# Gate and up products of both feed-forward stages as seven block products for eight, and a down product over all eight PSUM banks

## The chip, the cores and the metric

The kernel runs on one core of one Trainium2 chip. The metric is the device time of one execution in microseconds (us). Engines are called as the profile calls them: PE is TensorE, PEld its weight loads, DVE VectorE, ACT ScalarE, POOL GpSimd, SP the engine whose queue starts the transfers. A difference of less than 0.3% of the time (3.3 us) can't be told from none.

## The reference

One residual block on 512 tokens of width 1024: a feed-forward stage, a mixer of two kinds, and a second feed-forward stage. The change touches both feed-forward stages.

```
D_MODEL = 1024; SEQ = 512; D_FF = 2816
def swiglu(x, w_gu, w_down):
    gu = x @ w_gu                               # (512 x 1024) @ (1024 x 5632)
    gate, up = gu[..., :D_FF], gu[..., D_FF:]
    return (jax.nn.silu(gate) * up) @ w_down    # (512 x 2816) @ (2816 x 1024)

x = x + 1/2 * post1(SwiGLU_1(pre1(x)))
h = pre_mix(x); p = h @ w_in                    # RWKV-7 heads and a conv module on p
x = x + post_mix(concat(A, B) @ w_out)
x = x + 1/2 * post2(SwiGLU_2(pre2(x)))
```

All norms are RMS norms over the 1024 channels with a gain. Everything is float32.

## The kernel before

**Precision by three products.** Every float32 operand of a large product is split into a high part (rounded by ScalarE's cast) and a low part (VectorE: the operand minus its high part). `mm3` (L119) issues three matmuls for a block of 128 contraction rows: high with high (L121), low weight with high (L124), high weight with low (L125). All weights are in DRAM as blocks of 128x1024 float32 (512 KB). `wload` (L80) has SP's queue fetch one, in one fixed order for the whole program; `wblock` (L89) splits it: the cast on ACT (L97), the subtraction on DVE (L100).

**A feed-forward stage** (`ffn`, L286) has gate and up products of 22 column blocks each. The first four blocks (two of gate, two of up) go through `token_halves` (L262), with matmuls over 256 tokens, because the transposed tokens `hT` arrive in pieces. The other 40 blocks have eight contraction steps of three matmuls each, 24 matmuls over all 512 tokens for a block. After a gate and its up block, `tail` takes silu of the gate from PSUM (ACT, L294), multiplies by the up product (DVE, L295) and splits the result into high and low (ACT L297, DVE L298); all 22 split results stay in SBUF in the pool `g`.

**The down product** contracts over 22 blocks of 128. It goes over the tokens' four tiles with 512 output columns at a time: first output half over all 22 blocks, then the second half over 14; the last eight blocks (`NS = 8`) of the second half are done one token tile after the other, so that the tile's post work can start: `Post.piece` takes the sum of squares of a half on ACT (L132) and the scaled half on DVE (L240 to L244), `rs` works out the root on DVE (L49 to L54), and `add` (L251) adds to the residual x. x stays in SBUF. In the first stage the next operand `hT` is transposed tile by tile in between.

**Buffers.** Weight blocks have two raw, two high and two low buffers. Blocks that are fetched ahead of their stage (the first blocks of the mixer, the second half of `w_out`, the first blocks of the second feed-forward stage) have raw buffers of their own: four of tag `raw2`, or a tile of the pool `g`, of which there are 22. PSUM's eight banks are three of A, three of B, two of C and D together.

**Order.** A scheduler orders each engine's instructions at build time, by priorities that follow the program's text; each engine then runs its own list strictly in order. SP's list of weight fetches is fixed by `load` (L72). `w_out` does its first output half, fetches and splits four blocks for the second, posts the first half, fetches and splits the first four blocks of the second feed-forward stage, and then goes over the token tiles.

## Time and profile before

| | |
|---|---|
| median of 3 runs | 1094.14 us (1092.67 to 1096.12) |
| the profiled execution | 1087.74 us |
| its span in the trace | 1085.4 us |
| mean granted clock of TensorE | 0.969 of full speed |
| PE / DVE / ACT / POOL busy | 1030.7 / 530.7 / 408.4 / 147.3 us |
| weights and other data read | 94.50 MB, at 92 GB/s over the span |

The stages in the span, by where their first matmuls start: first feed-forward stage, gate and up, to 256; its down product to about 376, with the turn to the mixer; mixer to about 680; `w_out` to about 715; second stage, gate and up, to 958; its down product to the end. In the two gate and up stretches and in the down products PE is busy the whole time. In a row of a timeline the first number is the start in us and the second the duration; "x2" means that two instructions stand in one row. The end of a matmul is modelled, so the pitch from one start to the next is what is to be read.

### The profile page before, as it was taken

The numbers are of one execution on the slowest core, as the hardware profiler recorded it, in microseconds if no ns is written. First come the engines' busy times: TensorE is split into PE (matmuls) and PEld (weight loads), VectorE is DVE, ScalarE is ACT, GpSimd is POOL, SyncE is SP. The second block draws the span as 40 slices with busy tenths as digits, with TensorE's granted clock in tenths as the row PEclk, the third lists the DMA queues.
The fourth block names the chain that finished last, engine by engine and source line by source line (L and its number), as shares of the span: only waits on it lengthen the run. The fifth ranks groups of instructions, "written<-read, shape, count | busy, mean of one in ns | idle before, by whom it ended". The sixth has DMA issues, their size and how long they took to land.

```text
span 1085.4 us, 15405 instructions
## 1 busy us (share of the span) xinstructions
PE 1030.7 (95%) x6274; PEld 852.5 (79%) x6274; DVE 530.7 (49%) x1011; ACT 408.4 (38%) x628; POOL 147.3 (14%) x170
## 2 busy tenths in 40 slices
PE   8999999999999999859897788999999999999997
PEld 8888888888888797647676666888888888888885
DVE  5333333333224658879469797853333333332225
ACT  7322222222123446765346275543222222221221
POOL 0000000000000234693008280120000000000000
PEclk9999999999999999969896789999999999999999
DMA  6223232333336122121430330502333233333331
GB/s 233 71 89 105 91 103 88 105 90 105 95 97 225 59 72 61 58 70 59 81 98 20 59 118 21 194 20 78 97 98 97 97 97 98 98 97 97 98 116 78
DMA packets 52846, 101.27 MB, mean 93 GB/s; under 512 B 28584, under 2 KB 28712, under 8 KB 52776
## 3 DMA queue, kind: packets, MB, share of 16 engines
q1 hardware_dynamic: 51912, 97.67, 28.7%
q10 hardware_dynamic: 864, 2.63, 0.8%
q8 instruction: 49, 0.80, 0.3%
q14 instruction: 21, 0.17, 0.1%
HBM read 94.50 MB, written 5.78 MB: 92 GB/s over the span
## 4 chain that ended last, share of the span: by engine, by line
PE 72%; DVE 13%; ACT 4%; POOL 4%; DMA 3%; issue 3%; SPq 1%; DVEq 0%; ACTq 0%; POOLq 0%
PE ps L125 23%; PE ps L121 23%; PE ps L124 23%; POOL cacc L516 4%; DVE wlo L100 1%; DVE ps L682 1%; DVE stmp L679 1%; DMA td<-T 1%; DVE x L251 1%; ACT ms_j L132 1%; DMA N<-md 1%; DMA md<-Mt 1%; DVE rs_w L50 1%; ACT cpr L515 1%; ACT whi L97 1%
## 5 line engine op out<-in xcount | busy, mean ns | idle before, releaser
L121 PE MATMUL ps<-hT,whi 128*128 128x512 f32 (+1 forms) x888 | 339.4, 383 | 5.1 <-ACT hT L171 2.8
L124 PE MATMUL ps<-hT,wlo 128*128 128x512 f32 (+1 forms) x888 | 339.3, 382 | 1.5 <-DVE wlo L100 1.1
L125 PE MATMUL ps<-hT,whi 128*128 128x512 f32 (+1 forms) x888 | 339.2, 383 | 1.2 <-DVE hT L172 1.0
L100 DVE TENSOR_TENSOR wlo<-wraw,whi 128x1024 fp32r<-128x1024 f32 x141 | 174.1, 1236 | 318.6 <-ACT whi L97 318.3
L97 ACT CAST whi<-wraw 128x1024 fp32r<-128x1024 f32 x141 | 148.0, 1050 | 301.8 <-PE ps L125 181.4
L121 PEld LDWEIGHTS ps<-hT,whi 128*128 128x128 f32 x888 | 168.6, 190 | 43.5 <-issue 4.8
L125 PEld LDWEIGHTS ps<-hT,whi 128*128 128x128 f32 x888 | 168.3, 190 | 36.6 <-issue 3.7
L124 PEld LDWEIGHTS ps<-hT,wlo 128*128 128x128 f32 x888 | 168.7, 190 | 34.0 <-DVE wlo L100 1.9
L516 POOL TENSOR_TENSOR cacc<-cacc,cpr 128x192 f32<-128x192 f32 (+3 forms) x120 | 116.2, 968 | 46.4 <-ACT cpr L515 38.2
L121 PE MATMUL ps<-whi,g 128*128 128x512 f32 x288 | 112.0, 389 | 0.0
L124 PE MATMUL ps<-whi,g 128*128 128x512 f32 x288 | 112.0, 389 | 0.0
L125 PE MATMUL ps<-wlo,g 128*128 128x512 f32 x288 | 104.4, 389 | 0.0
L294 ACT ACTIVATE sg<-ps 128x512 f32<-128x512 f32 x44 | 26.4, 600 | 166.0 <-PE ps L125 166.0
L295 DVE TENSOR_TENSOR sg<-sg,ps 128x512 f32<-128x512 f32 x44 | 30.3, 688 | 111.5 <-PE ps L125 111.5
L515 ACT ACTIVATE cpr<-gpad,vecs 128x192 f32<-128x192 f32 (+3 forms) x120 | 68.0, 575 | 33.5 <-POOL cacc L516 33.3
L154 POOL TENSOR_TENSOR fg<-x,gain 128x1024 f32<-128x1024 f32 x8 | 19.1, 2388 | 434.7 <-DVE x L251 430.2
L125 PEld LDWEIGHTS ps<-wlo,g 128*128 128x128 f32 x288 | 54.1, 188 | 11.3
L121 PEld LDWEIGHTS ps<-whi,g 128*128 128x128 f32 x288 | 54.1, 188 | 11.3
L124 PEld LDWEIGHTS ps<-whi,g 128*128 128x128 f32 x288 | 54.1, 188 | 11.1
L508 DVE SCALAR_TENSOR_TENSOR ps<-gpad,vecs,ps 128x320 f32<-128x320 f32 (+2 forms) x87 | 40.6, 466 | 1.4
L298 DVE TENSOR_TENSOR g<-sg,g 128x512 fp32r<-128x512 f32 x44 | 30.2, 685 | 1.4 <-ACT g L297 1.4
L297 ACT CAST g<-sg 128x512 fp32r<-128x512 f32 x44 | 27.0, 615 | 5.5 <-DVE sg L295 5.5
(212 smaller groups left out, 1090.6 us busy)
## 6 DMA issues: line engine op xcount, KB each, us to landing
wraw<-w SPq DMA_DIRECT2D x145, 512.0 KB, 3.5
lraw<-w SPq DMA_DIRECT2D x17, 512.0 KB, 5.2
gain<-gains ACTq DMA_DIRECT2D x5, 512.0 KB, 4.5
x<-x SPq DMA_DIRECT2D x4, 512.0 KB, 5.0
xs<-x SPq DMA_DIRECT2D x4, 512.0 KB, 2.7
x<-xs SPq DMA_DIRECT2D x4, 512.0 KB, 7.2
out<-x SPq DMA_DIRECT2D x3, 512.0 KB, 2.6
N<-md SPq DMA_DIRECT2D x4, 256.0 KB, 4.1
```

The costliest lines, as they stand in the source:

```text
L97: c.last_hi = nc.scalar.copy(hi, raw)
L100: c.last_lo = nc.vector.tensor_tensor(lo, raw, hi, ALU.subtract)
L121: i = nc.tensor.matmul(out, lhsT=lh, rhs=rh, start=start, stop=False)
L124: nc.tensor.matmul(out, lhsT=ll, rhs=rh, start=False, stop=False)
L125: return nc.tensor.matmul(out, lhsT=lh, rhs=rl, start=False, stop=stop)
L294: nc.scalar.activation(sg, psg, AF.Silu)
L295: nc.vector.tensor_tensor(sg, sg, psu, ALU.mult)
L297: nc.scalar.copy(g[:, 0], sg)
L298: nc.vector.tensor_tensor(g[:, 1], sg, g[:, 0], ALU.subtract)
L508: self.dve_queue(nc.vector.scalar_tensor_tensor(dst, gp[:, j : j + n], dw[:, j : j + 1], lo, ALU.mult, ALU.add), False)
L515: nc.scalar.mul(pr, gp[:, n + j : j + SEQ], dw[:, j : j + 1])
L516: self.pool_queue(nc.gpsimd.tensor_tensor(hi, hi, pr, ALU.add), j == 1)
```

## The change

**Gate and up.** From the fifth column block on (`LEADF = 4` pairs of gate and up stay as they were, that is the first eight blocks), the blocks go in units of two: a pair of gate blocks, then a pair of up blocks. Two column blocks, two halves of the contraction and two halves of the tokens make a product of 2x2 by 2x2 blocks, which `Unit` does in seven block products for eight (Winograd's form of Strassen's scheme). A unit has 7 products of 4 contraction steps of three matmuls, 84 matmuls over 256 tokens, in place of 48 over 512. A stage has 18 such units.

On the weights' side a unit takes four sums (`S1` to `S4`, DVE, 128x512 each), splits four of its operands by wide instructions (1024 columns: block r0, sums, differences) and one by a narrow one (`a22`). On the tokens' side `Combos` makes four sums of quarters of `hT` once for a stage (10 additions of 128x1024 and 4 splits). Out of PSUM, `run` puts the seven products together with one copy on ACT and five additions on DVE (256, 512, 256, 256 and 512 columns). Silu and the product of gate and up are then done for two blocks at once (1024 columns), and the result is kept in float32 rather than split.

**Down.** All eight PSUM banks are accumulators (4 token tiles by 2 output halves), so one pass over the 22 blocks is enough, with 24 matmuls over 512 columns for each. A block's weights are now 128 contraction rows by 1024 outputs. The split of the SwiGLU result is made here (`split`, ACT and DVE, 512 columns for a block). `NS = 4`: the last four blocks are done token tile by token tile, for both output halves (24 matmuls for a tile, as before), and both halves' `piece` are now inside that loop.

**Buffers.** The pools of tiles are replaced by `SLOTS`. `raw2` has two buffers instead of four, and the blocks of the second half of `w_out` and the first blocks of the second stage, which had tiles of the pool `g` for their raw data, now go through `raw2` as well. x no longer stays in SBUF over a feed-forward stage: it is fetched again during the down product, in the second stage from a copy `xs2` that is stored at the end of `w_out`. The gains are fetched later. In the mixer, new settings (`O_SC`, `T_PR` and others) have the values that leave its order of instructions to the scheduler as it was; that order shifts a little all the same.

The number of bytes of weights is the same.

```diff
+SLOTS = {"g": 12, "s34": 4, "s12": 2, "sr": 2, "a22": 1, "sg": 2, "tmp": 2, "raw2": 2}
...
+class Combos:
...
+        def keep(n, x):
+            nc.scalar.copy(self.t[:, n, 0], x)
+            nc.vector.tensor_tensor(self.t[:, n, 1], x, self.t[:, n, 0], ALU.subtract)
...
+        sub(d, q(0, 1, 1), q(0, 0, 1))
+        sub(e, q(1, 1, 1), q(1, 0, 1))
+        add(d, d, e)
+        keep(2, d)
...
+class Unit:
...
+        r0, r1 = wload(c, i), wload(c, i + 1, "raw2")
...
+        add_eng.tensor_tensor(S1, r1[:, H[0]], r1[:, H[1]], ALU.add)
+        add_eng.tensor_tensor(S3, r0[:, H[0]], r1[:, H[0]], ALU.subtract)
+        wh, wl = wblock(c, i, raw=r0, aprev=aprev)
+        nc.vector.tensor_tensor(S2, S1, r0[:, H[0]], ALU.subtract)
+        nc.vector.tensor_tensor(S4, r0[:, H[1]], S2, ALU.subtract)
...
+        nc.scalar.copy(dh, dif)
+        nc.vector.tensor_tensor(dl, dif, dh, ALU.subtract)
+        nc.scalar.copy(sh, sums)
+        nc.vector.tensor_tensor(sl, sums, sh, ALU.subtract)
+        nc.scalar.copy(a22[:, 0], r1[:, H[1]])
...
+        nc.vector.tensor_tensor(a22[:, 1], r1[:, H[1]], a22[:, 0], ALU.subtract)
...
+    def mm(self, out, w, x):
+        h, l = self.w[w]
+        for k in range(4):
+            ks = slice(k * P, k * P + P)
+            mm3(self.c, out, h[:, ks], l[:, ks], x(0, k), x(1, k), k == 0, k == 3)
+
+    def run(self, n):
...
+        self.mm(pa[:, 0], "a11", cb.b(0, 0))
+        self.mm(pa[:, 1], "s2", cb.t_(1))
+        nc.scalar.copy(u[:, 3], pa[:, 0])
+        tt(u[:, 0], u[:, 3], pa[:, 1], ALU.add)
+        self.mm(pb[:, 0], "s1", cb.t_(0))
+        self.mm(pb[:, 1], "s3", cb.t_(2))
+        tt(u[:, 1:3], u[:, 0:1].broadcast_to([P, 2, 256]), pb, ALU.add)
+        self.mm(pd[:, 0], "a12", cb.b(1, 0))
+        tt(u[:, 0], u[:, 3], pd[:, 0], ALU.add)
+        tt(u[:, 3], u[:, 2], pb[:, 0], ALU.add)
+        self.mm(pc[:, 0], "s4", cb.b(1, 1))
+        self.mm(pc[:, 1], "a22", cb.t_(3))
+        tt(u[:, 1:3], u[:, 1:3], pc, ALU.add)
+        return u
...
+    for k in range(NF - NS):
+        w = wblock(c, wd + k)
...
+        g = split(k, "sg")
         for t in range(NT):
+            for h in range(2):
+                step(k, g, w, t, h)
...
+    for t in range(NT):
+        for h in range(2):
+            for k, g, w in last:
+                i = step(k, g, w, t, h, i)
+            q = posts[t].piece(h * 512, acc[t][h])
+        posts[t].rs()
+        i = finish(t, posts[t], i, q)
...
-    ws = preload(c, [wbase + 4 + kb for kb in W_ORDER], RAW_WS, own=0)
+    ws = preload(c, [wbase + 4 + kb for kb in W_ORDER], "raw2", own=0)
...
-                lws.extend(preload(c, range(B2, B2 + 4), RAW_F2, own=OWN_F2, prev=j, aprev=i))
+            lws.extend(preload(c, range(B2, B2 + 4), "raw2", own=OWN_F2, prev=j, aprev=i, home=("tmp", "sg")))
```

**Where instructions now stand.** On DVE, in the middle of the first stage's gate and up products, before: the split of a weight block (L100) and the tail of a pair (L295, L298) take turns.

```order
L100 TENSOR_TENSOR wlo<-wraw,whi 128x1024
L295 TENSOR_TENSOR sg<-sg,ps 128x512
L100 TENSOR_TENSOR wlo<-wraw,whi 128x1024
L298 TENSOR_TENSOR g<-sg,g 128x512
L100 TENSOR_TENSOR wlo<-wraw,whi 128x1024
```

After, the same engine over most of one unit (`s_...` are the sums of weights; `dlo`, `slo` and `a_...` the low parts of differences, sums and a22; `u` is what is put together out of PSUM; L108 is the subtraction that was L100):

```order
L387 TENSOR_TENSOR u<-u,ps 128x512
L354 TENSOR_TENSOR s_1384<-wraw,s_1383 128x512
L361 TENSOR_TENSOR slo<-s_1383,shi 128x1024
L389 TENSOR_TENSOR u<-u,ps 128x256
L364 TENSOR_TENSOR a_1395<-lraw,a_1395 128x512
L350 TENSOR_TENSOR s_1505<-lraw 128x512
L390 TENSOR_TENSOR u<-u,ps 128x256
L359 TENSOR_TENSOR dlo<-s_1384,dhi 128x1024
L353 TENSOR_TENSOR s_1505<-s_1505,wraw 128x512
L393 TENSOR_TENSOR u<-u,ps 128x512
L108 TENSOR_TENSOR wlo<-wraw,whi 128x1024
L351 TENSOR_TENSOR s_1506<-wraw,lraw 128x512
```

The additions out of PSUM of one unit (L384 to L393) stand between the sums and splits of the next unit and the one after it.

On SP, the fetches from the end of the mixer into the second feed-forward stage, before (eight `lraw` are the blocks fetched ahead: four of `w_out`, four of the second stage):

```order
L699 DMA Mt<-rd 32x16x32 x2
L74 DMA wraw<-w 128x1024 x2
L74 DMA lraw<-w 128x1024 x8
L74 DMA x<-xs 128x1024 x4
L74 DMA wraw<-w 128x1024 x62
L1052 DMA out<-x 128x1024 x3
```

After:

```order
L855 DMA Mt<-rd 32x16x32 x2
L74 DMA wraw<-w 128x1024 x2
L74 DMA lraw<-w 128x1024 x8
L74 DMA x<-xs 128x1024 x4
L74 DMA wraw<-w 128x1024 x2
L1198 DMA xs_78<-x 128x1024 x4
L74 DMA wraw<-w 128x1024 x3
L74 DMA lraw<-w 128x1024
```

The order of the fetches is the same, but the eight `lraw` now share two buffers, so that each waits until an earlier one has been split; the four stores of `xs2` stand behind the sixth block of the second stage (four `lraw`, two `wraw`), and from the ninth block on the fetches alternate between `wraw` and `lraw`.

On DVE, at the end of the first stage's down product, before (L244 x4 are the first halves of the four token tiles, L240 begins the post of the first tile's second half):

```order
L100 TENSOR_TENSOR wlo<-wraw,whi 128x1024
L100 TENSOR_TENSOR llo<-lraw,lhi 128x1024
L244 SCALAR_TENSOR_TENSOR fg<-ps,gain 128x512 x4
L100 TENSOR_TENSOR wlo<-lraw,whi 128x1024
L100 TENSOR_TENSOR llo<-lraw,lhi 128x1024
L100 TENSOR_TENSOR wlo<-lraw,whi 128x1024
L240 TENSOR_TENSOR ms_s<-ms_s 128x1
L244 SCALAR_TENSOR_TENSOR fg<-ps,gain 128x512
L49 TENSOR_SCALAR rs_y<-ms_s 128x1
```

After (L250 and L252 are the first half of the first tile, L248 and L252 its second half):

```order
L108 TENSOR_TENSOR wlast<-lraw,wlast 128x1024 x2
L108 TENSOR_TENSOR wlo<-lraw,whi 128x1024 x2
L108 TENSOR_TENSOR llo<-lraw,lhi 128x1024
L250 TENSOR_SCALAR ms_s<-ms_s 128x1
L252 SCALAR_TENSOR_TENSOR fg<-ps,gain 128x512
L248 TENSOR_TENSOR ms_s<-ms_s 128x1
L252 SCALAR_TENSOR_TENSOR fg<-ps,gain 128x512
L49 TENSOR_SCALAR rs_y<-ms_s 128x1
```

The first half's piece of a tile moved from ahead of the loop over the tiles into it.

## Rows read from the trace of the kernel before

**Rows 1.** Part 1 of the page: busy us (share of span), instructions, by engine.

```profile
PE 1030.7 (95%) x6274; PEld 852.5 (79%) x6274; DVE 530.7 (49%) x1011; ACT 408.4 (38%) x628; POOL 147.3 (14%) x170
```

**Rows 2.** Part 4 of the page: the chain that ended last, by engine.

```profile
PE 72%; DVE 13%; ACT 4%; POOL 4%; DMA 3%; issue 3%; SPq 1%; DVEq 0%; ACTq 0%; POOLq 0%
```

**Rows 3.** Windows: stretch, then PE, PEld, DVE, ACT, POOL busy (count), PEclk, DMA, GB/s.

```profile
38.40:60.10 21.70, 21.70 (x98) 17.98 (x97) 6.34 (x7) 5.27 (x7) 0.00 (x0) 1.00 0.27 85
60.10:256.00 195.90, 195.90 (x866) 162.24 (x866) 67.33 (x72) 56.02 (x72) 0.00 (x0) 1.00 0.31 97
256.00:354.00 98.00, 98.00 (x434) 81.19 (x433) 31.10 (x32) 27.37 (x33) 0.00 (x0) 1.00 0.40 131
354.00:400.00 46.00, 44.19 (x277) 39.34 (x276) 28.54 (x80) 19.10 (x31) 11.22 (x12) 1.00 0.14 52
...
763.50:959.00 195.50, 195.50 (x864) 161.96 (x863) 67.25 (x72) 55.69 (x73) 0.00 (x0) 1.00 0.31 97
```

**Rows 4.** Timeline, VectorE (start us, us, line), up stage: two SwiGLU products.

```profile
103.87 0.69 DVE L295 TENSOR_TENSOR sg<-sg,ps 128x512 f32<-128x512 f32 x1 [2.59 <-PE ps L125]
...
114.75 0.69 DVE L295 TENSOR_TENSOR sg<-sg,ps 128x512 f32<-128x512 f32 x1 [2.58 <-PE ps L125]
```

**Rows 5.** Timeline, TensorE: the last token halves, then the first 512-column product.

```profile
29.25 0.28 PE L125 MATMUL ps<-hT,whi 128*128 128x256 f32 x1
29.37 0.28 PE L121 MATMUL ps<-hT,whi 128*128 128x256 f32 x1
...
38.37 0.40 PE L121 MATMUL ps<-hT,whi 128*128 128x512 f32 x1
```

**Rows 6.** Timeline, VectorE, mixer stretch where it has a queue of work.

```profile
503.00 0.69 DVE L578 TENSOR_TENSOR ta<-ta,k 128x512 f32<-128x512 f32 x1
503.60 0.29 DVE L682 TENSOR_TENSOR ps<-ps,stmp 128x126 f32<-128x126 f32 x1
503.80 0.75 DVE L576 SCALAR_TENSOR_TENSOR bk<-tk,vecx,u 128x512 f32<-128x512 f32 x1
...
505.26 1.22 DVE L100 TENSOR_TENSOR wlo<-wraw,whi 128x1024 fp32r<-128x1024 f32 x1
506.39 0.75 DVE L352 SCALAR_TENSOR_TENSOR tk<-ps,vecs,tk 128x511 f32<-128x511 f32 x1
...
512.20 0.75 DVE L629 TENSOR_TENSOR ZT<-ps,maskS 128x256 f32<-128x256 f32 x2
512.86 0.27 DVE L682 TENSOR_TENSOR ps<-ps,stmp 128x110 f32<-128x110 f32 x1
...
513.78 0.25 DVE L679 TENSOR_TENSOR stmp<-N,ps 128x96 f32<-128x96 f32 x1
514.07 0.27 DVE L682 TENSOR_TENSOR ps<-ps,stmp 128x96 f32<-128x96 f32 x1
```

**Rows 7.** Groups by line, 60 to 256 us: count, busy us, mean ns.

```profile
L100 DVE TENSOR_TENSOR wlo<-wraw,whi 128x1024 fp32r<-128x1024 f32 x36 | 44.1, 1226 | 82.0 <-ACT whi L97 82.0
L97 ACT CAST whi<-wraw 128x1024 fp32r<-128x1024 f32 x36 | 37.8, 1049 | 69.2 <-PE ps L125 69.2
L295 DVE TENSOR_TENSOR sg<-sg,ps 128x512 f32<-128x512 f32 x18 | 12.4, 688 | 46.6 <-PE ps L125 46.6
L298 DVE TENSOR_TENSOR g<-sg,g 128x512 fp32r<-128x512 f32 x18 | 12.3, 685 | 0.0
```

**Rows 8.** Timeline, ScalarE: the sum of squares of one output half.

```profile
359.55 0.60 ACT L132 ACTIVATE ms_j<-ps 128x512 bf16<-128x512 f32 x1 [4.61 <-PE ps L125]
```

**Rows 9.** Timeline, VectorE, w_out: low parts, then the first tile's post.

```profile
681.14 4.62 DVE L100 TENSOR_TENSOR llo<-lraw,lhi 128x1024 fp32r<-128x1024 f32 x4
...
693.66 2.35 DVE L100 TENSOR_TENSOR llo<-lraw,lhi 128x1024 fp32r<-128x1024 f32 x2
695.94 0.15 DVE L240 TENSOR_TENSOR ms_s<-ms_s 128x1 f32<-128x1 f32 x1
```

**Rows 10.** DMA issues, 640 to 740 us: queue, count, KB each, us to landing.

```profile
lraw<-w SPq DMA_DIRECT2D x4, 512.0 KB, 4.1
```

More of the change, by code (lines that the diff above doesn't have):

```diff
@@ L83, in wload @@
     else:
-        raw = c.gp.tile([P, 1024], F32, name="lraw", tag=tag, bufs=NF if tag == "g" else NRAW2)
+        raw = slot(c, [P, 1024], F32, "lraw", tag)
     load(c, raw, c.A["w"][i])
@@ L271, in token_halves, with preload @@
                 turn.turn(i)
-def preload(c, blocks, tag, raws=(), own=2, prev=None, aprev=None):
+def preload(c, blocks, tag, raws=(), own=2, prev=None, aprev=None, home="g"):
     ws = []
@@ new lines, with ffn_down, split, step @@
+NS = 4
+LEADF = 4
+def ffn_down(c, wbase, gs, gpost, scale, finish, xin, ahead=None):
+    nc = c.nc
+    wd = wbase + 2 * NF
+    acc = [[psum(c, [P, 512], t) for t in tt] for tt in T_DOWN]
+    def split(k, tag="g"):
+        g = slot(c, [P, 2, 512], F32R, "gh", tag)
+        nc.scalar.copy(g[:, 0], gs[k])
+        nc.vector.tensor_tensor(g[:, 1], gs[k], g[:, 0], ALU.subtract)
+        return g
+    def step(k, g, w, t, h, prev=None):
+        return mm3(c, acc[t][h], g[:, 0, t * P : t * P + P], g[:, 1, t * P : t * P + P],
+                   w[0][:, h * 512 : h * 512 + 512], w[1][:, h * 512 : h * 512 + 512], k == 0, k == NF - 1, prev)
+    for k in range(NF - NS):
+        w = wblock(c, wd + k)
+        if k >= X_AT and (k - X_AT) % 2 == 0 and (k - X_AT) // 2 < NT:
+            xin((k - X_AT) // 2)
+        g = split(k, "sg")
+        for t in range(NT):
+            for h in range(2):
+                step(k, g, w, t, h)
+    big = c.gp.tile([P, NS, 2, 1024], F32R, name="wlast", tag="big")
+    last = []
+    for n in range(NS):
+        k = NF - NS + n
+        last.append((k, split(k), wblock(c, wd + k, big[:, n, 0], big[:, n, 1], wload(c, wd + k, "raw2"))))
+    posts = [Post(c, gpost, scale) for _ in range(NT)]
+    if ahead is not None:
+        ahead(None, None)
+    i = None
+    for t in range(NT):
[5 more added lines that the diff above has]
+        i = finish(t, posts[t], i, q)
@@ L600, in prep @@
         shift(c, psv, v["mu_v"][:, h1], v["o_v"][:, h1], vt)
-        self.scores(hp, z)
-        pv = self.ps([P, 8, 64], "B")
+        with self.later(O_SC[hp]):
+            self.scores(hp, z)
+        tc = c.tc
+        tc.cur_priority += O_PV[hp]
+        pv = self.ps([P, 8, 64], T_PR[2])
         for cc in range(8):
@@ L945, in body @@
                 raws.append(wload(c, t - 1))
-        raws += [wload(c, i, "g") for i in (2, 3)]
+        raws += [wload(c, i, "raw2") for i in (2, 3)]
         turn = Turn(c, new_ht(), T_PRE1, gcol)
@@ L961, in body @@
             turn.act(nc.scalar.mul(turn.xn[t], x[t], turn.y[t]))
-        gpo, gpr = gain(c, 1, turn.last), gain(c, 2, turn.last)
+        gs = ffn_up(c, 0, ws, turn, c.gp, "big")
+        x = [slot(c, [P, D], F32, "x", "s34") for _ in range(NT)]
+        gpo, gpr = gain(c, 1), gain(c, 2)
         turns, lws = [], []
@@ L975, in fin, with ahead @@
             return between(tn, t, i, x[t], gpr, post.fg)
-        ffn(c, 0, ws, turn, gpo, 0.5, fin, lambda i, j: lws.extend(preload(c, range(NB_FFN, NB_FFN + len(LEAD)), RAW_LEAD)))
+        def ahead(i, j):
+            lws.extend(preload(c, range(NB_FFN, NB_FFN + len(LEAD)), "raw2", home="g"))
+        ffn_down(c, 0, gs, gpo, 0.5, fin, lambda t: load(c, x[t], A["x"][t * P : t * P + P, :]), ahead)
         led = [psum(c, [P, SEQ], tag) for tag in LEAD]
@@ L991, in body @@
                 prio = marks[at]
-            with m.at(tc.cur_priority if prio is None else prio) if prio is not None else ExitStack():
+            late = 0
+            if op != "c" and "/" in arg:
+                arg, late = arg.split("/")
+            with m.at(prio) if prio is not None else m.later(int(late)) if late else ExitStack():
                 if op == "c":
@@ L1073, in host_layout @@
     a = {k: np.asarray(v) for k, v in inputs.items()}
-    gu = [f + s * NF for f in range(NF) for s in range(2)]
+    gu = [f + s * NF for f in range(LEADF) for s in range(2)] + [f + s * NF for p in range(LEADF, NF, 2) for s in range(2) for f in (p, p + 1)]
+    rows = lambda w: w.reshape(NF, P, D)
     win = []
     for st in PLAN.split():
-        st = st.split("@")[0]
+        st = st.split("@")[0].split("/")[0]
         if st[0] == "c":
```

203 lines of the change are left out of this document (119 added, 84 removed).

## Prediction

> **What bounds the kernel now.** I read the busy shares first: TensorE is busy for 1030.7 us of a span of 1085.4 us, VectorE for half of it [rows 1], and the chain that ended last is 72% TensorE and 13% VectorE [rows 2]. The share is an average, so I read the windows next. In both gate and up stretches, the place of the change, PE is busy in every microsecond, at a granted clock of 1.00, while DVE has work for 67 us of 196 and ACT for 56 [rows 3]. The same holds in the down product (98.00 of 98 us); only its end, with the post of the token tiles, leaves PE idle (44.19 of 46 us) [rows 3]. So a matmul saved in the gate and up products is time saved, as long as DVE, which is given nearly all the new work, does not become the longer of the two. Everything below turns on these two sums for one unit.
>
> **TensorE for one unit.** Before, two column blocks are 48 matmuls over 512 columns. Two SwiGLU products, one per pair of blocks, start at 103.87 and 114.75 us [rows 4], 10.88 us apart, thus 0.2267 us for a matmul. After, a unit is 84 matmuls over 256 columns. Their pitch is in the trace, since the token halves already use this shape with the same kinds of operands: 0.12 us from one to the next, and the 76 steps from 29.25 us to the first 512-column matmul at 38.37 us take 9.12 us [rows 5], 0.120 us each. The unit takes 84 x 0.120 = 10.08 us. Halving the columns costs 6% a column (0.240 for 0.227 us), so of the eighth that Strassen's scheme saves about half is left: 10.88 - 10.08 = 0.80 us a unit, and with 18 units in each of two stages 28.8 us.
>
> The rule that speaks against halving the columns is on the weight side. The rows show that a new set of weights for each 256-column matmul fits into 0.120 us [rows 5]. The Trainium skill, "TensorE: Matmul & The Clock Gate", section "LDWEIGHTS (loading the stationary operand)", puts a weight load at columns/1.2 ns, an estimate of 107 ns for these 128 columns; laid end to end with the matmul's own 0.11 us by its section "Back-to-back issue gap", that would make an estimate of 0.216 us each and the change a loss of some 260 us. The trace disagrees with an end-to-end reading: the load is hidden.
>
> **VectorE for one unit.** Ten and a half wide instructions and three narrow ones now stand against 10.08 us. Seven have 512 columns (four sums, the low part of a22, two of the additions out of PSUM), three have 1024 (the low parts of block, sums and differences), three 256 (the other additions), and every second unit has one SwiGLU product of 1024, half of one per unit. What an instruction costs on a full queue is its pitch, not its duration. Where DVE has a queue of work, an instruction of 512 starts the next one 0.60 us later though it lasts 0.69, one of 1024 after 1.13, two of 256 that read PSUM after 0.66 [rows 6]. I take 0.60, 1.14 and 0.33: 7 x 0.60 + 3 x 1.14 + 3 x 0.33 + 0.57 = 9.18 us. A neighbour that needs the result just written waits longer: 0.29 us for 96 columns against 0.20 for 126 columns [rows 6]; two such neighbours a unit add 0.2 us. Reading PSUM adds next to nothing (688 ns for the product out of PSUM, 685 for the one out of SBUF [rows 7]). So DVE needs about 9.4 of 10.08 us, and PE stays the bound, with 0.7 us to spare. ACT has five casts and copies and half a silu, under 6 us at 1049 ns for 1024 columns [rows 7].
>
> A sum below the bound isn't enough, since DVE runs strictly in order and waits on PE in mid-unit. The tightest place is the addition out of PSUM after the s1 and s3 products (L387): behind it stand the last weight sum of the next unit (L354), its `slo` (L361), and in every second unit the wide SwiGLU product (L438). That is 0.60 + 0.60 + 1.14 + 1.14 = 3.5 us after s3. PE meanwhile has s4, a22 and the next unit's a11 and mostly a12, 48 matmuls or 5.8 us (36 and 4.3 where a12 is already done), before it needs `slo`. Slack 0.8 to 2.3 us: no wait.
>
> **Start of the units.** `Combos` adds 14 wide DVE instructions, 16 us, where DVE had 6.34 us of work in 21.70 [rows 3]. They and the first unit's sums end about when PE has done the four leading pairs. Between no wait and 2 us a stage; I take 0.5, as PE has the first a11 and a12 (2.9 us) to do before it needs a sum. Twice 0.5 is +1.0.
>
> **Down product.** As many matmuls (22 blocks x 24) over the same 512 columns. The split of the SwiGLU result moves here: 0.60 us of DVE and as much of ACT per block of 5.44 us, in a stretch where DVE has 31 us of 98 [rows 3]. Cost 0, and the gate and up stretch loses the two narrow instructions a pair that it had. The fetches of x add four blocks to 22 per stage, at a DMA share of 0.40 before [rows 3]: 0.
>
> **End of the first down product.** Both pieces of a tile now fall in its own turn. ScalarE's sum of squares takes 0.60 us [rows 8], and DVE's scaling another 0.60 [rows 6]. The first half's is done while PE does the second half's 12 matmuls (2.7 us), but DVE and ACT are what the turn waits on there, and the blocks of the mixer's start now have two raw buffers for seven. From 0 (all beside PE) to 3 us (0.7 for each of four tiles); I take +1.5. The end of the second stage has no turn behind it: 0.
>
> **w_out into the second stage.** Here two `raw2` buffers stand for eight fetches. Before, all eight had landed ahead of need; the fourth low part of the first group starts at 681.14 us and the whole group ends by about 685.7, the last low parts of the second stage's first blocks start at 693.66, and right behind them in DVE's order comes the post of the first tile, at 695.94 [rows 9], from which the turn follows. After, blocks three and four can only be fetched when one and two are split (682.3 and 683.4); a fetch takes 4.1 us to land [rows 10], a cast and a low part 1.05 and 1.14, so they are split at about 689. The next pair lands near 693 and is split near 696, the last pair lands near 699 and is split at 701.4, and only then comes the post, 5.4 us later than 695.94. PE has work from the second half of the tiles meanwhile but waits on the turn: +4.5 us. The bounds are 2 (the fetches overlap with the splits better) and 7 (each pair waits its whole 4.1 us and the x fetches queue behind).
>
> **Sum.** -28.8 + 1.0 + 1.5 + 4.5 = -21.8 us on the profiled execution, 1087.74 to 1065.9. The mixer's slight reordering I leave at 0, within 3 us either way. The median of the runs stands 0.59% above the profiled execution; so the forecast is 1072 us. Its own range is 1062 (no loss at the joints: 1058.9 on the profiled execution, 1065 as a median, and the mixer's 3 us) to 1079 (both joints and the starts at their upper ends).
>
> **Rivals.** *DVE becomes the bound, still faster.* If in this mix each instruction costs its duration, as where each needs the one before it, a unit is 7 x 0.69 + 3.5 x 1.226 + 3 x 0.42 = 10.4 us [rows 6, 7], 0.49 less than before; 17.6 - 7.0 = 10.6 us gained, 1083 us. For it: the sums and the additions form chains. Against: pitches in a mixed queue were the shorter ones [rows 6]. The Trainium skill, "VectorE: DVE Perf Modes", section "The DRAIN you can't avoid", states this rule, that the next instruction does not start until the pipe has emptied; the trace shows a start 0.09 us ahead of the end, so it doesn't hold for independent neighbours. 15%.
>
> *Slower: DVE's order holds up PE.* The place is L387 with `slo` behind it. If DVE runs at full durations and its waits on PE and on ACT's casts (a22 has one buffer, s1 and s2 two) leave holes, PE waits for `slo` in each unit, DVE waits for PE, and the unit is DVE's sum plus the holes. With 1 us of holes it is 11.4: 36 x 0.52 + 7 = +26 us, 1120. It decides from 10.69 us a unit, 10.88 less the 7 us of the joints over 36 units. For it: 0.7 us of slack in 10. Against: 0.8 to 2.3 us between `slo` and its use. 11%.
>
> *The 256-column pitch doesn't last.* If weights of many tiles slow it from 0.120 to 0.130 us, 84 x 0.01 x 36 = 30 us go and the result is about 1102. For it: weight loads are busy for most of the time already (162 of 196 us) [rows 3], with half the columns to hide behind. Against: 9 us at 0.120 without a break [rows 5]. 6%.
>
> *Weight loads end to end with matmuls* once none has 512 columns to hide behind: a load is busy for 162.24/866 = 0.187 us [rows 3], so a unit would take 84 x (0.120 + 0.187) = 25.8 us, 14.9 more than before, and the kernel about 1640 us. Against: the pitch of 0.120 [rows 5] has a load in it. 2%.
>
> **How the numbers follow.** Forecast 66%, the rivals 15, 11, 6 and 2. Faster by over 0.3% (under 1090.9): all of the first two, 81%. Within 0.3%: the tail of either, 5%, out of the slower and pitch cases. Slower: 14%. The range takes in the forecast and most of DVE as the bound: 1062 to 1088.
>
> **What would show it.** In the gate and up stretch: PE's pitch at 0.120 us; 10.08 us from one unit's SwiGLU to the next; PE idle near 0 and DVE at 93 to 100%. If PE idles there behind `slo` or `dlo`, the DVE sum was wrong. At `w_out`, the first tile's post 5 us behind its second half's last matmul rather than at once; at the first down product's end the same four turns, each up to 0.7 us later. It would be made wrong by a wait I haven't priced that returns in every unit: 0.6 us of it takes 22 us.

## The result and the profile after

The changed kernel takes 1099.75 us (median of 11 runs, 1097.12 to 1102.56) against 1090.37 us before (11 runs), a ratio of 1.0082 (95% interval 1.0062 to 1.0102): slower by 0.8%, where 1072 us were forecast. Its profiled execution has a span of 1095.2 us against 1085.4.

Where the time went is read from the starts of TensorE's matmuls in the two traces. The first 512-column product, the first product of the down stage, the first `wa,wup` product (a small product that stands for the mixer's start here), the first product of w_out's second half and the same marks of the second stage cut the span into stretches:

| stretch (by TensorE's matmuls), us | before | after | difference |
|---|---|---|---|
| start to the first 512-column product | 38.37 | 38.88 | +0.51 |
| first stage, gate and up | 217.63 | 203.22 | -14.41 |
| its down product, to the mixer's first wa,wup product | 152.87 | 156.59 | +3.72 |
| mixer and w_out's first half | 280.60 | 310.16 | +29.56 |
| w_out's second half, to the second stage's first 512-column product | 51.10 | 56.10 | +5.00 |
| second stage, gate and up | 217.62 | 203.22 | -14.40 |
| its down product, to the last matmul | 119.46 | 119.48 | +0.02 |

The gain came to the tenth of a microsecond, the two joints (where one stage hands over to the next) cost 8.7 us where 6.0 had been forecast, and a stage that the change was said to leave alone, the mixer, lost more than the whole gain.

The page of the changed kernel, part 1 and the first line of part 4, answers to [rows 1, 2]. VectorE's share rose from 49% to 72%, TensorE's hardly moved:

```profile
PE 1034.7 (94%) x7570; PEld 907.0 (83%) x7570; DVE 785.2 (72%) x1417; ACT 488.0 (45%) x726; POOL 147.2 (13%) x170
...
PE 75%; DVE 13%; ACT 4%; DMA 3%; issue 3%; POOL 2%; SPq 1%; DVEq 0%; ACTq 0%; POOLq 0%
```

Windows of the changed kernel (columns as in [rows 3]): in the gate and up stretches TensorE is busy throughout, with 1538 records in 188 us where it had 866 in 195.9, and VectorE for 171 us. From 400 to 690 us, mostly mixer, the granted clock is 0.83:

```profile
62.00:250.00 188.00, 188.00 (x1538) 186.65 (x1537) 170.96 (x247) 84.82 (x104) 0.00 (x0) 1.00 0.34 107
...
354.00:400.00 46.00, 42.13 (x259) 36.72 (x258) 27.80 (x74) 20.42 (x34) 14.06 (x24) 0.96 0.20 68
400.00:690.00 290.00, 250.90 (x2394) 186.21 (x2393) 210.84 (x493) 148.69 (x258) 120.48 (x135) 0.83 0.21 53
...
763.50:959.00 195.50, 195.50 (x1546) 191.73 (x1545) 182.76 (x254) 88.30 (x105) 0.00 (x0) 1.00 0.34 108
```

TensorE in the middle of a unit, after, answers to [rows 5]: the 256-column products of sums follow each other at 0.120 us.

```profile
146.10 0.28 PE L133 MATMUL ps<-tsum,shi 128*128 128x256 f32 x1
146.22 0.28 PE L129 MATMUL ps<-tsum,shi 128*128 128x256 f32 x1
146.34 0.28 PE L132 MATMUL ps<-tsum,slo 128*128 128x256 f32 x1
```

VectorE over most of a unit, after, answers to [rows 4] and [rows 6]: 1024 columns start the next instruction after 1.13 us, 512 after 0.60, 256 after 0.33, and the waits between (in brackets) are short:

```profile
148.22 0.69 DVE L387 TENSOR_TENSOR u<-u,ps 128x512 f32<-128x512 f32 x1 [0.35 <-PE ps L133]
148.83 1.22 DVE L361 TENSOR_TENSOR slo<-s,shi 128x1024 fp32r<-128x1024 f32 x1
149.96 1.22 DVE L438 TENSOR_TENSOR g<-sg,u 128x1024 f32<-128x1024 f32 x1
151.10 1.22 DVE L108 TENSOR_TENSOR wlo<-wraw,whi 128x1024 fp32r<-128x1024 f32 x1
152.23 0.41 DVE L389 TENSOR_TENSOR u<-u,ps 128x256 f32<-128x256 f32 x1
152.56 1.22 DVE L359 TENSOR_TENSOR dlo<-s,dhi 128x1024 fp32r<-128x1024 f32 x1
153.70 0.69 DVE L350 TENSOR_TENSOR s<-lraw 128x512 f32<-128x512 f32 x1
154.30 0.69 DVE L364 TENSOR_TENSOR a<-lraw,a 128x512 fp32r<-128x512 f32 x1
...
158.54 1.23 DVE L108 TENSOR_TENSOR wlo<-wraw,whi 128x1024 fp32r<-128x1024 f32 x1 [1.09 <-ACT whi L105]
```

### The profile page after: what moved, and what is told of

It is laid out like the page before. It is cut to its first block, busy times and chain, and to the rows that moved or that the text cites. A ratio compares the mean times of both kernels' runs of the same rounds, so it can differ in the third digit from the quotient of the medians.

```text
span 1095.2 us, 18642 instructions
## 1 busy us (share of the span) xinstructions
PE 1034.7 (94%) x7570; PEld 907.0 (83%) x7570; DVE 785.2 (72%) x1417; ACT 488.0 (45%) x726; POOL 147.2 (13%) x170
## 4 chain that ended last, share of the span: by engine, by line
PE 75%; DVE 13%; ACT 4%; DMA 3%; issue 3%; POOL 2%; SPq 1%; DVEq 0%; ACTq 0%; POOLq 0%
PE ps L129 24%; PE ps L132 23%; PE ps L133 23%; POOL cacc L666 2%; DMA lraw<-w 1%; PE ps L797 1%; DVE ps L658 1%; DVE x L259 1%; DVE ps L837 1%; DVE stmp L834 1%; DVE E L917 1%; ACT whi L105 1%; DVE rs_w L50 1%; DVE wlo L108 1%; DVE SV L935 1%
## 5 line engine op out<-in xcount | busy, mean ns | idle before, releaser
L108 DVE TENSOR_TENSOR wlo<-wraw,whi 128x1024 fp32r<-128x1024 f32 x105 | 129.6, 1234 | 136.9 <-ACT whi L105 136.5
L129 PE MATMUL ps<-hT,whi 128*128 128x256 f32 (+1 forms) x600 | 201.9, 338 | 8.1 <-ACT hT L179 4.2
L132 PE MATMUL ps<-hT,wlo 128*128 128x256 f32 (+1 forms) x600 | 199.6, 334 | 1.4 <-DVE wlo L108 1.4
L133 PE MATMUL ps<-hT,whi 128*128 128x256 f32 (+1 forms) x600 | 199.1, 334 | 0.7 <-DVE hT L180 0.4
L129 PEld LDWEIGHTS ps<-hT,whi 128*128 128x128 f32 x600 | 117.3, 196 | 23.7 <-ACT hT L179 5.2
L133 PEld LDWEIGHTS ps<-hT,whi 128*128 128x128 f32 x600 | 116.9, 196 | 13.6 <-issue 2.7
L133 PE MATMUL ps<-wlo,gh 128*128 128x512 f32 x288 | 112.0, 389 | 0.0
L132 PE MATMUL ps<-whi,gh 128*128 128x512 f32 x288 | 112.0, 389 | 0.0
L132 PE MATMUL ps<-tsum,slo 128*128 128x256 f32 x288 | 80.0, 283 | 0.0
L133 PE MATMUL ps<-tsum,shi 128*128 128x256 f32 x288 | 80.0, 283 | 0.0
L129 PE MATMUL ps<-tsum,shi 128*128 128x256 f32 x288 | 76.3, 283 | 0.0
L129 PE MATMUL ps<-whi,gh 128*128 128x512 f32 x288 | 71.5, 389 | 0.0
L133 PEld LDWEIGHTS ps<-wlo,gh 128*128 128x128 f32 x288 | 54.1, 188 | 11.2
L132 PEld LDWEIGHTS ps<-whi,gh 128*128 128x128 f32 x288 | 54.1, 188 | 11.2
L129 PEld LDWEIGHTS ps<-whi,gh 128*128 128x128 f32 x288 | 53.9, 188 | 11.1
L133 PEld LDWEIGHTS ps<-tsum,shi 128*128 128x128 f32 x288 | 55.3, 192 | 0.0
L132 PEld LDWEIGHTS ps<-tsum,slo 128*128 128x128 f32 x288 | 55.3, 192 | 0.0
```

The lines of the kernel that those rows point to most:

```text
L108: c.last_lo = nc.vector.tensor_tensor(lo, raw, hi, ALU.subtract)
L129: i = nc.tensor.matmul(out, lhsT=lh, rhs=rh, start=start, stop=False)
L132: nc.tensor.matmul(out, lhsT=ll, rhs=rh, start=False, stop=False)
L133: return nc.tensor.matmul(out, lhsT=lh, rhs=rl, start=False, stop=stop)
```

## The experiments

### What slowed the mixer

The mixer's text differs between the two kernels in one place that does something: its call of `scores` is wrapped in `later(0)`. That context adds 0 to the priority counter and, at its end, sets the counter to one above where it stood at the beginning, so what is issued behind `scores` has the same priorities as `scores` itself.

**e1_plain_scores** takes that out of the changed kernel:

```diff
-        with self.later(O_SC[hp]):
-            self.scores(hp, z)
+        self.scores(hp, z)
```

> The changed kernel with one edit: the call of `scores` in the mixer is no longer wrapped in `later(0)`, which leaves the priority counter at one above where `scores` began, so that what the mixer issues after it gets the same early priorities as `scores` itself. Theory 1 (this reset made the scheduler interleave score products with projection products): the mixer, from the first wa,wup product to the first w_out product 242.7 us in the changed kernel and 220.2 before, comes back to 217 to 224 us, and the whole to 1075 to 1081 us. Theory 2 (the mixer is slower because the first feed-forward stage now hands over its operands later and from other buffers): the mixer stays at 240 us or more and the whole at about 1100 us. In both the gate and up stretches stay as they are, 14.4 us shorter each than before.

Measured: 1089.52 us, 0.9989 of before (0.9973 to 1.0005), so 10 us back, half of what theory 1 said. The stretch of mixer and w_out's first half takes 303.6 us (280.6 before, 310.2 after). Gate and up are 203.22 us again. Neither theory holds as it was put: up to the first w_out product the mixer takes 225.5 us, near what theory 1 said, but from there to w_out's second half 78.0 us where the kernel before takes 60.4.

**e2_before_later** puts the same wrapping into the kernel before.

```diff
-        self.scores(hp, z)
+        with self.later(0):
+            self.scores(hp, z)
```

> The kernel before with that one edit put in: `scores` wrapped in `later(0)`, nothing else of the change. Theory 1: the mixer loses 15 to 25 us, the whole goes from 1090 to about 1110 us. Theory 2: no change, 1090 us within 3.

Measured: 1112.81 us, 1.0202 of before (1.0175 to 1.0229). One wrapped call, with no change to the feed-forward stages, costs 22 us. That is theory 1, and it is not symmetric: put in, 22 us are lost; taken out, 10 come back. The place is the same in both kernels that have the wrapping. Of the second pair of heads, the score products (what `scores` issues on TensorE: L643 before, L797 after, 64 columns each) follow each other in the kernel before. TensorE's timeline there, before:

```profile
475.36 0.49 PE L643 MATMUL ps<-E,bk 64*64 64x64 f32 x8
475.57 0.49 PE L643 MATMUL ps<-I,bk 64*64 64x64 f32 x8
475.78 0.49 PE L643 MATMUL ps<-E,bk 64*64 64x64 f32 x8
```

They begin at 473.96 and the last starts at 478.92 us, 70.0 us after the first `wa,wup` product. In the changed kernel they alternate, two by two, with the products of the next projection (512 columns):

```profile
471.19 0.79 PE L132 MATMUL ps<-hT,wlo 128*128 128x512 f32 x1
471.92 0.47 PE L797 MATMUL ps<-I,bk 64*64 64x64 f32 x2
472.32 0.79 PE L133 MATMUL ps<-hT,whi 128*128 128x512 f32 x1
473.04 0.47 PE L797 MATMUL ps<-I,bk 64*64 64x64 f32 x2
473.45 0.79 PE L129 MATMUL ps<-hT,whi 128*128 128x512 f32 x1
```

One projection product and its two score products take 1.13 us (471.19 to 472.32), and the last scores start at 498.48 us, 99.8 us after the first `wa,wup` product: 29.7 us later than before. In e2_before_later it is 99.5 us. That this is nearly the stretch's 29.56 us is chance: the delay does not stay the same. The third pair's last scores are 18.4 us late (130.5 against 112.1 us after the mark), the first w_out product 22.5 us and the start of w_out's second half 29.56; and in e2_before_later the same 29.5 us of delay goes with a stretch longer by only 23.0 us. The window of this place, after, and the one behind it: TensorE busy in all of 30 us, at a granted clock of 0.51, the level of 1.2 GHz, with VectorE at 11 us of 30; then the clock is back at 1.00:

```profile
464.00:494.00 30.00, 30.00 (x169) 17.62 (x167) 11.35 (x30) 7.59 (x12) 12.94 (x10) 0.51 0.23 58
494.00:512.00 18.00, 18.00 (x79) 11.60 (x79) 12.85 (x27) 11.93 (x18) 10.37 (x9) 1.00 0.11 30
```

The same group of one projection and two score products, there at full clock, takes 0.68 us:

```profile
494.44 0.49 PE L129 MATMUL ps<-hT,whi 128*128 128x512 f32 x1
494.86 0.32 PE L797 MATMUL ps<-E,bk 64*64 64x64 f32 x2
495.12 0.49 PE L132 MATMUL ps<-hT,wlo 128*128 128x512 f32 x1
```

VectorE's longest wait there, among those from 460 to 512 us, is for these scores:

```profile
DVE LU L799 <- PE ps L797: 12.0, 1, 12.0
```

The order of the changed kernel, which can be read without running it, shows the same thing (TensorE, second pair of heads; L129 to L133 are the projection; each score line stands for two products, as the trace has them from 463.7 to 466.9 us):

```
L132 MATMUL ps<-hT,wlo 128x512
L797 MATMUL ps<-I_3962,bk 64x64
L133 MATMUL ps<-hT,whi 128x512
L797 MATMUL ps<-I_3962,bk 64x64
L129 MATMUL ps<-hT,whi 128x512
L132 MATMUL ps<-hT,wlo 128x512
L133 MATMUL ps<-hT,whi 128x512
L797 MATMUL ps<-E,bk 64x64
```

In e1_plain_scores this place is healthy again (the last scores start 70.4 us after the first `wa,wup` product), but another one is not: the second triangular solve, whose last step on VectorE (L684 before, L838 there) starts 201.5 us after that product before, and 224.1 us after it in e1_plain_scores, and in the 56.5 us ahead of it VectorE now does the eight output steps of the first heads (L964, L965), which it did behind it before, six root steps (L67) for three, and 34 convolution steps (L658) for 29. These rows show where the 22.6 us have gone by then, not how they add up. So theory 3: order alone is the loss, of which the wrapping is one part, and the scheduler, given other instructions upstream, makes another order of the same text.

**f1_after_old_order** and **f2_before_new_order** exchange the orders. The mixer and w_out's first half issue the same instructions in the same sequence in both kernels' texts (1560 on TensorE, 517 on VectorE, 269 on ScalarE, 156 on GpSimd), so the order of one can be held in the other by an edge (an order without a wait) from each instruction to the next of its engine:

```diff
+def keep_order(c, n0):
...
+    ins, at = c.nc.cur_bb.bb.instructions[n0:], 0
+    for eng in ("PE", "DVE", "Activation", "Pool"):
+        own = [i for i in ins if str(i.engine).endswith(eng)]
+        rank = order[at : at + len(own)]
+        at += len(own)
+        for a, b in zip(rank, rank[1:]):
+            c.tc.add_manual_dep(own[b], own[a].name, mybir.DependencyInfo(mybir.DependencyClass.NoSync, mybir.DependencyReason.DATA), reason="order")
...
+    keep_order(c, c.n0)
     acc0 = wo.acc
```

> The changed kernel, its feed-forward stages and joints untouched, with the instructions of the mixer and of w_out's first half held, on TensorE, VectorE, ScalarE and GpSimd, in the very order that they have in the kernel before (an order edge from each to the next of its engine). Theory 3 (the mixer's loss is its order alone): the stretch from the mixer's first wa,wup product to w_out's second half comes back from 310.2 to 279 to 283 us, and the whole to 1068 to 1074 us. Rival (the mixer is also slower because its operands, weights or buffers come later from the new first stage): the stretch stays at 290 us or more and the whole at 1080 or more.

> The kernel before with nothing changed but the order of the mixer and of w_out's first half, which is held in the order that the changed kernel has. Theory 3: the stretch from the first wa,wup product to w_out's second half goes from 280.6 to about 310 us and the whole from 1090 to 1115 to 1122 us. Rival: below 1105 us, if the new first stage's hand-over is part of the loss.

Measured: f1_after_old_order 1070.9 us, 0.9821 of before (0.9802 to 0.9839); f2_before_new_order 1116.33 us, 1.0240 (1.0218 to 1.0262). The change with the old order is faster by 1.8%, the old kernel with the new order slower by 2.4%. In the traces VectorE's instructions of this stretch follow each other, over all 509 rows of it, as in the kernel before in f1_after_old_order, and as in the changed kernel in f2_before_new_order. The stretch of mixer and w_out's first half, as one window each, before:

```profile
408.90:689.50 280.60, 241.03 (x2496) 187.73 (x2496) 223.34 (x511) 158.31 (x272) 120.64 (x135) 0.88 0.27 73
```

f1_after_old_order:

```profile
399.70:683.20 283.50, 243.05 (x2496) 189.17 (x2495) 222.73 (x509) 158.18 (x273) 120.78 (x135) 0.88 0.24 63
```

the changed kernel:

```profile
398.70:708.90 310.20, 269.98 (x2496) 200.88 (x2495) 222.31 (x509) 158.11 (x273) 120.48 (x135) 0.83 0.22 58
```

the kernel before with the new order:

```profile
408.90:718.30 309.40, 268.28 (x2495) 200.20 (x2495) 222.49 (x509) 157.74 (x272) 120.53 (x135) 0.83 0.25 69
```

The orders carry their time with them: 280.6 (before), 283.5, 310.2, 309.5 us (by the marks of the table). VectorE, ScalarE and GpSimd are busy for the same time in all, TensorE for 27 us longer in the bad order, where the granted clock is 0.83 instead of 0.88. The rival of f1_after_old_order keeps at most 2.9 us for the hand-over from the new first stage, and hardly that: with the same order held, the stretch takes 281.0 to 282.8 us in the four runs further on that build on it. How much of the loss is the low clock, and how much the order at full clock, these runs don't separate; at this one place, 30 us at 0.68 us a group in place of 1.13 would be some 18 us (an estimate from the two rows).

### The joints

**e3_four_raw** is e1_plain_scores with four raw buffers for the fetches around w_out:

```diff
-        ws.append(wblock(c, i, hi, lo, raws[n] if n < len(raws) else wload(c, i, tag), prev, aprev))
+        ws.append(wblock(c, i, hi, lo, raws[n] if n < len(raws) else wload(c, i, tag[n] if isinstance(tag, tuple) else tag), prev, aprev))
...
-    ws = preload(c, [wbase + 4 + kb for kb in W_ORDER], "raw2", own=0)
+    ws = preload(c, [wbase + 4 + kb for kb in W_ORDER], ("raw2", "raw2", "sr", "sr"), own=0)
...
-            lws.extend(preload(c, range(B2, B2 + 4), "raw2", own=OWN_F2, prev=j, aprev=i, home=("tmp", "sg")))
+            lws.extend(preload(c, range(B2, B2 + 4), ("raw2", "raw2", "sr", "sr"), own=OWN_F2, prev=j, aprev=i, home=("tmp", "sg")))
```

> As e1_plain_scores, and the four raw blocks of w_out's second half and the four first blocks of the second stage go through four buffers (two of tag raw2, two of the idle tag sr) instead of two. Theory (two buffers for eight fetches hold up the first tile's post in w_out, which cost about 5 us from the start of w_out's second half to the first 512-column product of the second stage): 3 to 6 us faster than e1_plain_scores, and that stretch as long as in the kernel before, 51 us. Rival (it is the later fetch of x, the stores of x or the later gains that hold it up): no change against e1_plain_scores.

Measured: 1082.36 us, 0.9922 of before (0.9902 to 0.9941), 7.2 us under e1_plain_scores; the stretch from w_out's second half to the second stage is 50.85 us (56.50 in e1_plain_scores, 51.10 before). The mixer's stretch was 1.6 us shorter as well, though its order is the same, so about 5.6 of the 7.2 us are the buffers'. **f3_four_raw_old_order** has the same edit on f1_after_old_order:

> e3_four_raw with the old order held as in f1_after_old_order: both losses taken out. Theory 3 with the four raw buffers: 5 us faster than f1_after_old_order, 1062 to 1068 us, the fastest so far; from the start of w_out's second half to the second stage's first 512-column product 51 us. If the gain of four buffers hangs on the mixer's order: as f1_after_old_order.

Measured: 1063.84 us, 0.9757 of before (0.9734 to 0.9780), the fastest kernel of the study, 7 us under f1_after_old_order; the joint takes 50.83 us. VectorE at this joint in the changed kernel, answering to [rows 9] (low parts of the last two pairs, then the first tile's post):

```profile
711.05 1.23 DVE L108 TENSOR_TENSOR wlo<-lraw,whi 128x1024 fp32r<-128x1024 f32 x1 [0.37 <-ACT whi L105]
713.79 1.23 DVE L108 TENSOR_TENSOR wlo<-lraw,whi 128x1024 fp32r<-128x1024 f32 x1 [1.51 <-ACT whi L105]
716.83 1.23 DVE L108 TENSOR_TENSOR llo<-lraw,lhi 128x1024 fp32r<-128x1024 f32 x1 [1.82 <-ACT lhi L105]
719.50 1.22 DVE L108 TENSOR_TENSOR llo<-lraw,lhi 128x1024 fp32r<-128x1024 f32 x1 [1.44 <-ACT lhi L105]
720.64 0.15 DVE L248 TENSOR_TENSOR ms_s<-ms_s 128x1 f32<-128x1 f32 x1
```

and in f3_four_raw_old_order:

```profile
682.09 2.36 DVE L108 TENSOR_TENSOR wlo<-lraw,whi 128x1024 fp32r<-128x1024 f32 x2 [0.18 <-ACT whi L105]
684.37 2.35 DVE L108 TENSOR_TENSOR llo<-lraw,lhi 128x1024 fp32r<-128x1024 f32 x2
686.64 0.15 DVE L248 TENSOR_TENSOR ms_s<-ms_s 128x1 f32<-128x1 f32 x1
```

With two buffers the last three low parts each wait 1.4 to 1.8 us for a cast that waits for a fetch, and the post stands behind the last: it comes 11.8 us after the start of w_out's second half (720.64 - 708.85). With four they come as [rows 9] shows them, and the post comes after 6.5 us (686.64 - 680.17), as before the change (695.94 - 689.47).

**f4_four_raw_down** gives the end of the first down product four raw buffers as well.

```diff
-        last.append((k, split(k), wblock(c, wd + k, big[:, n, 0], big[:, n, 1], wload(c, wd + k, "raw2"))))
+        last.append((k, split(k), wblock(c, wd + k, big[:, n, 0], big[:, n, 1], wload(c, wd + k, ("raw2", "raw2", "sr", "sr")[n]))))
...
-            lws.extend(preload(c, range(NB_FFN, NB_FFN + len(LEAD)), "raw2", home="g"))
+            lws.extend(preload(c, range(NB_FFN, NB_FFN + len(LEAD)), ("raw2", "raw2", "sr", "sr"), home="g"))
```

> As f3_four_raw_old_order, with four raw buffers instead of two for the seven blocks at the end of the first down product too. If the 3.7 us lost between the first down product's start and the mixer's first wa,wup product come from the second piece in each tile's post (theory): no change against f3_four_raw_old_order, 157 us for that stretch. If they come from two raw buffers for seven blocks: 2 to 4 us faster, about 153 us.

Measured: 1064.58 us, 0.9767 (0.9746 to 0.9788), no change; the stretch is 156.83 us (156.72). Buffers are not what costs the 3.7 us there. **f5_first_half_early** moves the first half's pieces out of the loop over the tiles; the last eight blocks then come through the two `wraw` buffers, and their halves are split one by one (not shown in the cut):

```diff
-    for k in range(NF - NS):
+    for k in range(NF - 2 * NS):
...
+        for t in range(NT):
+            mm3(c, acc[t][0], g[:, 0, t * P : t * P + P], g[:, 1, t * P : t * P + P], hi[:, 0:512], lo[:, 0:512], False, k == NF - 1)
+        last.append((k, g, n))
     posts = [Post(c, gpost, scale) for _ in range(NT)]
+    for t in range(NT):
+        posts[t].piece(0, acc[t][0])
...
     for t in range(NT):
-        for h in range(2):
-            for k, g, w in last:
-                i = step(k, g, w, t, h, i)
-            q = posts[t].piece(h * 512, acc[t][h])
+        for k, g, n in last:
+            i = mm3(c, acc[t][1], g[:, 0, t * P : t * P + P], g[:, 1, t * P : t * P + P], big[:, n, 0], big[:, n, 1], False, k == NF - 1, i)
+        q = posts[t].piece(512, acc[t][1])
```

> f3_four_raw_old_order with the down product's end arranged as in the kernel before: the first output half is done over all 22 blocks and its four pieces are taken ahead of the loop over the tiles, the loop has the last eight blocks of the second half alone (24 matmuls a tile, as many as with two halves of four blocks). Theory (the second piece in each tile's post lengthens the turn by about 0.7 us a tile): the stretch from the first down product's start to the first wa,wup product goes from 156.7 to 153 us, the whole to 1059 to 1062 us. Rival (x fetched again, or the later gains, hold up the first post): no change.

Measured: 1064.88 us, 0.9780 (0.9763 to 0.9797), no gain; the stretch is 157.24 us. The theory is half right. The additions of the residual (L259) of the four tiles, changed kernel:

```profile
348.42 1.28 DVE L259 SCALAR_TENSOR_TENSOR x<-fg,rs_y,x 128x1024 f32<-128x1024 f32 x1
...
354.98 1.29 DVE L259 SCALAR_TENSOR_TENSOR x<-fg,rs_y,x 128x1024 f32<-128x1024 f32 x1
...
362.62 1.28 DVE L259 SCALAR_TENSOR_TENSOR x<-fg,rs_y,x 128x1024 f32<-128x1024 f32 x1
...
370.20 1.29 DVE L259 SCALAR_TENSOR_TENSOR x<-fg,rs_y,x 128x1024 f32<-128x1024 f32 x1
```

and f5_first_half_early:

```profile
352.34 1.28 DVE L259 SCALAR_TENSOR_TENSOR x<-fg,rs_y,x 128x1024 f32<-128x1024 f32 x1
...
358.21 1.28 DVE L259 SCALAR_TENSOR_TENSOR x<-fg,rs_y,x 128x1024 f32<-128x1024 f32 x1
...
365.13 1.28 DVE L259 SCALAR_TENSOR_TENSOR x<-fg,rs_y,x 128x1024 f32<-128x1024 f32 x1
...
372.00 1.28 DVE L259 SCALAR_TENSOR_TENSOR x<-fg,rs_y,x 128x1024 f32<-128x1024 f32 x1
```

Spacing per tile is 6.6, 7.6 and 7.6 us with the second piece in the loop, 5.9, 6.9 and 6.9 without, as before the change: 0.7 us a tile, as the theory says. But the first tile's addition comes 110.7 us after the down product's start (352.34 - 241.68) instead of 106.3 (348.42 - 242.10), since the four first pieces and two splits for the mixer now stand right ahead of it on ScalarE and VectorE. The term is shown, the remedy isn't one. It is also not all of the 3.72 us: the first tile's addition is no later than before the change (106.2 us after the down product's start there), so the turns make three times 0.7, or 2.1 us. The other 1.6 us lie behind the last addition, from which to the first `wa,wup` product it is 28.5 us in the changed kernel and 26.9 before; in f5_first_half_early it is 26.9 again. What makes them is open.

### VectorE's room

**e4_one_more_dve** (on e1_plain_scores) and **f6_two_more_dve** (on f3_four_raw_old_order) take low parts in `Unit` twice, both that of the differences:

```diff
         nc.vector.tensor_tensor(dl, dif, dh, ALU.subtract)
+        nc.vector.tensor_tensor(dl, dif, dh, ALU.subtract)
```

and f6_two_more_dve that of the sums too:

```diff
         nc.scalar.copy(sh, sums)
+        nc.vector.tensor_tensor(sl, sums, sh, ALU.subtract)
         nc.vector.tensor_tensor(sl, sums, sh, ALU.subtract)
```

> As e1_plain_scores, with one more VectorE instruction of 1024 columns in every unit (the low part of the differences is taken twice), 36 in all, to see how much room VectorE has. By the pitches, 9.4 us a unit, it then needs 10.5 against TensorE's 10.08 us: 12 to 18 us slower than e1_plain_scores. If VectorE needs its full durations (10.4 a unit) or its place in the order already sets the unit: 36 x 1.14, about 40 us slower. If it has over a microsecond to spare in a unit: no change.

> f3_four_raw_old_order with two more VectorE instructions of 1024 columns in every unit (the low parts of differences and of sums are each taken twice). If VectorE needs the sum of its pitches, 9.2 us a unit as e4_one_more_dve's 208.03 us for a gate and up stretch gives, a unit now takes 9.2 + 2 x 1.14 = 11.5 us and a stretch of 18 units 203.2 + 18 x (11.5 - 10.08) = 229 us, the whole about 51 us over f3_four_raw_old_order. If e4_one_more_dve only lost to waits that one more instruction moved, and VectorE has more room than that: a stretch below 222 us.

Measured: e4_one_more_dve 1090.43 us, 0.9993 (0.9977 to 1.0009), as if VectorE had room. But its gate and up stretches take 208.03 us instead of 203.22, 9.6 us more in all (12 to 18 were expected), and its mixer's stretch 293.1 instead of 303.6, though not a letter of the mixer differs: the scheduler's order again (VectorE's rows there differ from those of e1_plain_scores from the 28th on), which hid the answer in the total. f6_two_more_dve (a single run, 1123.11 us, 59 us over f3_four_raw_old_order where 51 were expected) has the mixer's order held, and its stretches take 231.89 and 231.93 us. Windows of the gate and up stretch, e4_one_more_dve:

```profile
62.00:240.00 178.00, 176.27 (x1456) 174.85 (x1456) 177.50 (x248) 78.61 (x96) 0.00 (x0) 1.00 0.33 103
```

f6_two_more_dve:

```profile
62.00:260.00 198.00, 181.31 (x1434) 176.25 (x1434) 194.22 (x261) 76.75 (x93) 0.00 (x0) 0.98 0.29 90
```

and what TensorE waited for there, f6_two_more_dve:

```profile
PE ps L132 <- DVE slo L363: 13.0, 12, 2.0
PE ps L129 <- ACT dhi L358: 1.9, 4, 0.6
```

A unit takes 10.35 us with one more instruction (10.08 + 4.81/18) and 11.67 with two (10.08 + 28.67/18); less 1.14 and 2.28 that is 9.2 and 9.4 us for the unit as it is. The second figure has idle time of VectorE in it: it is busy for 194.22 of 198.00 us in f6_two_more_dve, 11.45 of 11.67, and so by its busy time the unit needs 9.2 there too. In the changed kernel VectorE is busy for 170.96 of 188.00 us, 9.2 of 10.08.

## Why the prediction was wrong

**The step that failed is "The mixer's slight reordering I leave at 0, within 3 us either way".** It was 29.56 us in the traces, and where the order was exchanged alone 28.9 us of the stretch and 26.5 us of the time (1116.33 against 1089.86). The step rested on the settings being neutral, as the text ahead of the prediction says of them. One of them, `later(0)`, is not: it resets the priorities behind `scores`, worth 22 us by itself (e2_before_later). And that the text is neutral would not have been enough, as e1_plain_scores against f1_after_old_order shows (1089.52 and 1070.9 us). Why the scheduler makes the orders that it makes stays open. The order could have been read beforehand, and the mixer's TensorE and VectorE rows compared with those before; no other term of the sum rested on anything so little looked at. The mixer is where TensorE idles (250.90 of 290 us in the window above) and VectorE's chain counts; that is where a moved row costs.

**TensorE per unit: right.** 0.80 us a unit and 28.8 us were forecast; 14.41 and 14.40 came, at the pitch of [rows 5]. No unit waited at the start, where 1.0 us had been put: the stretches are 18 x 0.80 us shorter to the hundredth. (The +0.51 us ahead of the first 512-column product is scatter: it comes at 38.2 to 38.5 us in all other kernels with the change.)

**VectorE per unit: right.** 9.18 to 9.4 us against 9.2 and 9.4 by two experiments. Pitches, not durations, are the price on a full queue, and where the queue was overfull TensorE waited at `slo` (f6_two_more_dve) and `dlo` (e4_one_more_dve), the places named for it. The Trainium skill, "VectorE: DVE Perf Modes", section "The DRAIN you can't avoid", has the rule that the next instruction starts only when the pipe is empty, and exempts from it an instruction that is not held. Without the exemption f6_two_more_dve's unit would be 10.4 + 2 x 1.23 = 12.8 us, an estimate from the durations; its trace shows 11.67.

**w_out into the second stage: right.** 4.5 forecast, 5.0 us measured, and four buffers give it back (50.83 us). The post was forecast 5.4 us later and came 5.3 us later. (Of [rows 9] the prediction says that the fourth low part starts at 681.14 us; that is the start of the first of the four. Its sum uses the row rightly.)

**End of the first down product: mis-sized.** 1.5 forecast with an upper end of 3 us, 3.72 measured (5.2 in f1_after_old_order). The mechanism, 0.7 us in a tile's turn, is the upper end of the bounds, and I had taken half of it without a reason from a row; it is there for three of the four tiles, 2.1 us. The rest, 1.6 us behind the last tile's addition, was in no term.

**Down product, end of the second stage: right**, 0 against 0.02 us.

**The rivals.** The one on the other side, VectorE's order holding up TensorE in the units, did not occur (no wait of TensorE from 62 to 250 us); the slower result came from a place that no rival named. With the old order held, f1_after_old_order takes 1070.9 us against the 1072 forecast. That this is so close is in part luck: its gain is 19.0 us (1089.86 - 1070.9) where about 22 were forecast, and the forecast stood on a median of three runs, 1094.14 us, which with more runs came to about 1090. So the sum was good for the gate and up products, low by some 3 us in all for the joints (8.7 against 6.0 us), and blind to the stage that the change only touches.

## What to carry to other kernels

Where a scheduler sets the order, a stage whose text a change leaves alone is not left alone: compare its rows engine by engine, above all where small products feed a chain, before giving it a cost of 0. A tuned order is worth holding with order edges when the stages around it are rewritten; here that turned a loss of 0.8% into a gain of 1.8%, and with four raw buffers 2.4%. Where a total does not move, look at the stretches: e4_one_more_dve lost 9.6 us in the two gate and up stretches and won 10.4 in the mixer.
